# The pool for masked scores in the attention core: 15 tiles instead of 11

## The chip, the cores and the metric

The kernel runs on one core of one Trainium2 chip. The core has TensorE (PE, matmuls, with a weight load PEld ahead of each), VectorE (DVE), ScalarE (ACT), GpSimd (POOL) and SyncE (SP, which here issues the DMAs). The metric is the device time of one execution in microseconds, the median of several runs.

## What is computed

Two sequences, of 2048 and 256 rows of width 1024, go through two layers and a last RMS norm. The first layer is windowed attention, the second a bidirectional mLSTM. The change touches the attention alone. In the reference, cut to that:

```python
kb, vb = band(k), band(v)                       # the block's own 128 keys and both neighbours'
s = einsum('bnqgrd,bnkgd->bngrqk', qb, kb) * HEAD_DIM ** -0.5
s = where(mask, s, -inf)
m = maximum(max(s, axis=-1), sink)
p = exp(s - m)
den = sum(p, axis=-1) + exp(sink - m)
o = einsum('bngrqk,bnkgd->bnqgrd', p / den, vb)
y = (o * silu(z)) @ w_out
```

There are 16 query heads in 4 groups, 4 key heads, heads of 64, and blocks of 128 queries: 16 blocks for the first sequence, 2 for the second.

## The kernel before

The rows are 18 tiles of 128 (`NT`). `attn_core` works through them: `front(t)` projects tile `t` (keys and values in `kv`, queries in two halves in `q`; each is 24 matmuls of 128x512 in `project`, L471 to L473), turns keys and queries by the rope products (L1126, L1128, on VectorE), transposes them on TensorE (L528, L546) and splits them into two parts for exact products (`KH` and `KL`, `Q`). `core(t)` computes the attention of block `t` in three interleaved generators:

- `scores`: for each group of 4 heads, two matmuls per head write a score bank `s` in PSUM (L595, L596; 2 banks). VectorE adds the mask, writes the sum to a tile `Sm` in SBUF and leaves the row maximum (L598). Then `nm` and `es` (L603, L605), and ScalarE turns each `Sm` into its exponential in place (L609).
- `transposes`: TensorE transposes each 128x128 part of the four `Sm` of a group into a bank `ptp` (L622; 2 banks); ScalarE or VectorE copies it out to `PT` (L625; 4 tiles).
- `values`: TensorE multiplies `PT` with the values into a bank `o` (L634; 1 bank), ScalarE copies it out (L642) and SyncE stores it.

An `Sm` tile comes from a ring of `NSM` tiles. A block with both neighbours has 16 of them, each read by 3 transpositions; a tile is free again after the last of these. The lines:

```python
NSM = 11
...
Sm = p.tile([128, 3, 128], F32, tag="Sm", name="Sm", bufs=NSM)
nc.vector.tensor_tensor_reduce(Sm[:, :nk], S[:, :nk], mask[:, t % 3, win, :], 1.0, MASKED,
                               ALU.add, ALU.max, mx[:, c:c + 1])
...
nc.scalar.activation(Sg[c][:, :nk], Sg[c][:, :nk], AF.Exp, bias=nm[:, c:c + 1],
                     scale=HD ** -0.5, accum_out=rs[:, c:c + 1])
...
nc.tensor.transpose(tp[:, c, :], Ss[g][c][:, j, :], self.ident[:])
```

The strings `AORDER`, `AORDER1` and `AORDER2` say in which turn the generators of a block and the `front` of the block after next are written down. The order on each engine's queue is not that of the code, though: the kernel is recorded with a scheduler (`schedule_with_timeline_sim=True`, L1199) that reorders it while it hands out tiles, and a pool's size is one of the things that it goes by. Each engine then runs its queue in order.

After the attention core, `attn_gate` computes the gate `z`. Its weights `w_z` are loaded and split while the last blocks of the attention run (`part`, L193 and L194; `combinations`, L225 to L234); the first pair of its tiles is multiplied plainly (`plain`, L414 to L416, called Z here: 48 matmuls for the first halves, then 48 for the second).

Of the kernel before, what the change touches and what calls it, by code (L numbers as in the profile page):

```python
# [42 lines left out]
XOPS = ("a11", "s2", "a12", "s3", "s1", "a22", "s4")  # L43
WOPS = ("b11", "t2", "b21", "t3", "t1", "t4", "b22")
PAIRS = [(t, t + 1) for t in range(0, NT, 2)]
NSM = 11
NPT = 4
SPT = 18
AORDER = "fffssssfsffffppsvppv"
# [15 lines left out]
class Trunk:  # L65
# [422 lines left out]
    def attn_core(self):  # L488
        nc, tc, a = self.nc, self.tc, self.a
        with ExitStack() as st:  # L490
# [83 lines left out]
            def core(t):  # L574
# [9 lines left out]
                def scores():  # L584
                    for g in range(KVH):
                        mx = p.tile([128, 4], F32, tag="mx", name="mx", bufs=3)
                        Sg = []
                        for c in range(GRP):
# [7 lines left out]
                            nc.tensor.matmul(S[:, :nk, :], q, KL[:, g, win, :], start=False, stop=True)  # L596
                            Sm = p.tile([128, 3, 128], F32, tag="Sm", name="Sm", bufs=NSM)
                            nc.vector.tensor_tensor_reduce(Sm[:, :nk], S[:, :nk], mask[:, t % 3, win, :], 1.0, MASKED,  # L598
# [605 lines left out]
```

## Time and profile before

| | us |
|---|---|
| median of 3 runs | 2272.67 (2269.81 to 2273.28) |
| the profiled execution, its time | 2262.48 |
| its span | 2260.7 |
| TensorE busy | 2188.9 (97%) |
| VectorE busy | 1555.5 (69%) |
| ScalarE busy | 1163.0 (51%) |
| GpSimd busy | 462.1 (20%) |

The attention core takes the first 702 us of the span. The other 1558 us are the gate, the output projection, the mLSTM projections and its core. A busy share of TensorE is read with care: the end of a matmul is modelled and overlaps the start of the next, so its real pace is in the distance from start to start. In a row of several instructions ("x8"), the time is from the first start to the last end. A weight load (PEld) may run ahead of its matmul, so its idle time is not always lost time.

### The profile page before, as it was taken

The numbers are of one execution on the slowest core, as the hardware profiler recorded it, in microseconds if no ns is written. First come the engines' busy times: TensorE is split into PE (matmuls) and PEld (weight loads), VectorE is DVE, ScalarE is ACT, GpSimd is POOL, SyncE is SP. The second block draws the span as 40 slices with busy tenths as digits, with TensorE's granted clock in tenths as the row PEclk, the third lists the DMA queues.
The fourth block names the chain that finished last, engine by engine and source line by source line (L and its number), as shares of the span: only waits on it lengthen the run. The fifth ranks groups of instructions, "written<-read, shape, count | busy, mean of one in ns | idle before, by whom it ended". The sixth has DMA issues, their size and how long they took to land.

```text
span 2260.7 us, 34007 instructions
## 1 busy us (share of the span) xinstructions
PE 2188.9 (97%) x11342; PEld 1759.3 (78%) x11342; DVE 1555.5 (69%) x3437; ACT 1163.0 (51%) x2627; POOL 462.1 (20%) x410
## 2 busy tenths in 40 slices
PE   8999999999989999999999999999999987999998
PEld 7767676666666888788888899978887866888887
DVE  7565656566787779766855844676696677777784
ACT  6454545455565335556733732556474455455553
POOL 4212121212001221232000000023222235433320
PEclk9999999999999999999999999999999997999999
DMA  7111110111214446766854854655686565765642
GB/s 271 49 39 50 34 54 35 50 38 45 89 61 168 149 150 219 233 210 211 291 177 165 291 175 143 209 187 185 200 263 213 182 221 211 229 199 193 215 159 71
DMA packets 190160, 358.02 MB, mean 158 GB/s; under 512 B 20992, under 2 KB 23840, under 8 KB 189984
## 3 DMA queue, kind: packets, MB, share of 16 engines
q1 hardware_dynamic: 189840, 355.83, 47.5%
q8 instruction: 90, 1.47, 0.3%
q14 instruction: 86, 0.70, 0.1%
q10 hardware_dynamic: 144, 0.01, 0.0%
HBM read 258.48 MB, written 97.28 MB: 157 GB/s over the span
## 4 chain that ended last, share of the span: by engine, by line
PE 79%; DVE 8%; ACT 5%; DMA 4%; issue 2%; POOL 2%; SPq 0%; DVEq 0%; POOLq 0%; ACTq 0%
PE pj L471 6%; PE pj L473 6%; PE pj L472 6%; PE pj L297 4%; PE pj L299 4%; PE pj L298 4%; PE c L338 4%; PE pj L338 4%; PE ptp L622 3%; PE o L634 3%; PE c L297 3%; PE c L298 3%; PE c L299 3%; PE d L299 3%; PE d L298 3%; PE d L297 3%
## 5 line engine op out<-in xcount | busy, mean ns | idle before, releaser
L126 ACT CAST xhi<-rawx 128x512 fp32r<-128x512 f32 x396 | 243.7, 618 | 446.8 <-PE c L338 94.2
L127 DVE TENSOR_TENSOR xlo<-rawx,xhi 128x512 fp32r<-128x512 f32 x362 | 267.6, 743 | 94.7 <-ACT xhi L126 88.3
L471 PE MATMUL pj<-whi,xhi 128*128 128x512 f32 x720 | 294.5, 411 | 9.2 <-ACT whi L171 5.5
L473 PE MATMUL pj<-whi,xlo 128*128 128x512 f32 x720 | 283.7, 402 | 3.5 <-DVE xlo L127 3.5
L472 PE MATMUL pj<-wlo,xhi 128*128 128x512 f32 x720 | 285.6, 397 | 0.0
L609 ACT ACTIVATE Sm<-Sm,nm 128x384 f32<-128x384 f32 (+1 forms) x288 | 167.1, 582 | 95.1 <-DVE nm L603 88.7
L297 PE MATMUL pj<-whi,xhi 128*128 128x512 f32 x480 | 192.2, 400 | 4.9 <-ACT whi L193 3.4
L298 PE MATMUL pj<-wlo,xhi 128*128 128x512 f32 x480 | 190.3, 397 | 0.0
L299 PE MATMUL pj<-whi,xlo 128*128 128x512 f32 x480 | 190.0, 396 | 0.0
L598 DVE CUSTOM_DVE_ANT_0 Sm<-s,mask 128x384 f32<-128x384 f32 (+1 forms) x272 | 136.1, 530 | 73.1 <-PE s L596 70.0
L471 PEld LDWEIGHTS pj<-whi,xhi 128*128 128x128 f32 x720 | 136.1, 189 | 44.1 <-issue 8.8
L473 PEld LDWEIGHTS pj<-whi,xlo 128*128 128x128 f32 x720 | 136.1, 189 | 41.5 <-issue 6.5
L472 PEld LDWEIGHTS pj<-wlo,xhi 128*128 128x128 f32 x720 | 136.1, 189 | 30.4 <-issue 2.4
L622 PE MATMUL ptp<-ident,Sm 128*128 128x128 f32 x800 | 135.5, 280 | 10.5 <-DVE PT L625 7.1
L622 PEld LDWEIGHTS ptp<-ident,Sm 128*128 128x128 f32 x800 | 94.5, 141 | 55.0 <-ACT Sm L609 19.1
L297 PE MATMUL c<-whi,xhi 128*128 128x512 f32 x320 | 127.6, 399 | 0.0
L297 PE MATMUL d<-whi,xhi 128*128 128x512 f32 x320 | 127.3, 398 | 0.0
L298 PE MATMUL c<-wlo,xhi 128*128 128x512 f32 x320 | 127.3, 398 | 0.0
L299 PE MATMUL c<-whi,xlo 128*128 128x512 f32 x320 | 127.0, 397 | 0.0
L299 PE MATMUL d<-whi,xlo 128*128 128x512 f32 x320 | 126.8, 396 | 0.0
L298 PE MATMUL d<-wlo,xhi 128*128 128x512 f32 x320 | 126.1, 394 | 0.0
L595 PE MATMUL s<-KH,Q 128*128 128x384 f32 (+1 forms) x288 | 106.1, 380 | 10.2 <-DVE mx L598 4.5
(260 smaller groups left out, 5431.8 us busy)
## 6 DMA issues: line engine op xcount, KB each, us to landing
rawx<-xn2T SPq DMA_DIRECT2D x120, 256.0 KB, 3.1
x<-x SPq DMA_DIRECT2D x108, 256.0 KB, 4.5
rawx<-xsum SPq DMA_DIRECT2D x96, 256.0 KB, 2.8
rawx<-xT SPq DMA_DIRECT2D x72, 256.0 KB, 3.1
raww<-w_oz SPq DMA_DIRECT2D x64, 256.0 KB, 4.4
v<-v SPq DMA_DIRECT2D x36, 258.0 KB, 2.4
rawx<-v SPq DMA_DIRECT2D x36, 258.0 KB, 2.8
rawx<-x SPq DMA_DIRECT2D x36, 256.0 KB, 2.8
```

The costliest lines, as they stand in the source:

```text
L126: nc.scalar.copy(hi[:], src)
L127: (eng or nc.vector).tensor_sub(lo[:], src, hi[:].bitcast(F32))
L297: nc.tensor.matmul(o, xh, wh, start=i == 0 and not more, stop=False, skip_group_check=more)
L298: nc.tensor.matmul(o, xh, wl, start=False, stop=False, skip_group_check=more)
L299: nc.tensor.matmul(o, xl, wh, start=False, stop=i == 3, skip_group_check=more)
L338: nc.tensor.matmul(p, x, w[:, c0:c1], start=first and i + j == 0, stop=last and i == len(ws) - 1 and j == 2, skip_group_check=True)
L471: nc.tensor.matmul(o[:, :n], xh, wh, start=kt == 0, stop=False)
L472: nc.tensor.matmul(o[:, :n], xh, wl, start=False, stop=False)
L473: nc.tensor.matmul(o[:, :n], xl, wh, start=False, stop=kt == KT - 1)
L598: nc.vector.tensor_tensor_reduce(Sm[:, :nk], S[:, :nk], mask[:, t % 3, win, :], 1.0, MASKED, ALU.add, ALU.max, mx[:, c:c + 1])
L609: nc.scalar.activation(Sg[c][:, :nk], Sg[c][:, :nk], AF.Exp, bias=nm[:, c:c + 1], scale=HD ** -0.5, accum_out=rs[:, c:c + 1])
L622: nc.tensor.transpose(tp[:, c, :], Ss[g][c][:, j, :], self.ident[:])
```

## The change

One constant: `NSM`, the number of tiles in the ring for masked scores and their exponentials, goes from 11 to 15. A tile is 1536 bytes in each partition.

```diff
-NSM = 11
+NSM = 15
```

The four tiles add 6144 bytes per partition to the pool `a1`; the `PT` tiles and the pool with `KH`, `KL` and the mask behind it move up by as much. The scheduler makes another order of the attention core, from about 112 us on. TensorE's queue shows it. The first place is a block in the steady run, around 350 us in the trace of before. Names with numbers are buffers: `ptp_3682` is the first bank of transposed exponentials of one group (`Sm_3501` to `Sm_3516`), `s_3788`, `s_3793` and `s_3811` are score banks of the next block. Before:

```order
L622 MATMUL ptp_3682<-ident_60,Sm_3506 128x128
L595 MATMUL s_3788<-KH_283,Q_3200 128x384
L596 MATMUL s_3788<-KL_284,Q_3200 128x384
L595 MATMUL s_3793<-KH_283,Q_3200 128x384
L596 MATMUL s_3793<-KL_284,Q_3200 128x384
L622 MATMUL ptp_3682<-ident_60,Sm_3511 128x128
L595 MATMUL s_3811<-KH_283,Q_3200 128x384
L596 MATMUL s_3811<-KL_284,Q_3200 128x384
L622 MATMUL ptp_3682<-ident_60,Sm_3516 128x128
L622 MATMUL ptp_3696<-ident_60,Sm_3501 128x128
```

Single transpositions of one group alternate with score matmuls of the next block. The same transpositions on TensorE after the change:

```order
L622 MATMUL ptp_3682<-ident_60,Sm_3501 128x128
L622 MATMUL ptp_3682<-ident_60,Sm_3506 128x128
L622 MATMUL ptp_3682<-ident_60,Sm_3511 128x128
L622 MATMUL ptp_3682<-ident_60,Sm_3516 128x128
L622 MATMUL ptp_3689<-ident_60,Sm_3468 128x128
L622 MATMUL ptp_3689<-ident_60,Sm_3473 128x128
L622 MATMUL ptp_3689<-ident_60,Sm_3478 128x128
L622 MATMUL ptp_3689<-ident_60,Sm_3483 128x128
L473 MATMUL pj_3752<-whi_351,xlo_3735 128x512
L471 MATMUL pj_3752<-whi_357,xhi_3734 128x512
```

The four of a group stand together, and a projection follows; 23 instructions stand between the last of these transpositions and the bank `ptp_3696`, and the scores `s_3788` and `s_3793` come after that.

The second place is the end of the attention core, on TensorE, up to the first gate matmul. Before:

```order
L622 MATMUL ptp<-ident,Sm 128x128 x11
L634 MATMUL o<-PT,V 64x512 x2
L595 MATMUL s<-KH,Q 128x256
L596 MATMUL s<-KL,Q 128x256
L595 MATMUL s<-KH,Q 128x256
L596 MATMUL s<-KL,Q 128x256
L622 MATMUL ptp<-ident,Sm 128x128
L634 MATMUL o<-PT,V 64x512 x2
L622 MATMUL ptp<-ident,Sm 128x128 x15
L634 MATMUL o<-PT,V 64x512 x4
```

And the same end on TensorE after:

```order
L634 MATMUL o<-PT,V 64x512 x2
L622 MATMUL ptp<-ident,Sm 128x128 x4
L595 MATMUL s<-KH,Q 128x256
L596 MATMUL s<-KL,Q 128x256
L622 MATMUL ptp<-ident,Sm 128x128 x12
L634 MATMUL o<-PT,V 64x512 x2
L622 MATMUL ptp<-ident,Sm 128x128 x2
L634 MATMUL o<-PT,V 64x512 x2
L622 MATMUL ptp<-ident,Sm 128x128 x10
L634 MATMUL o<-PT,V 64x512 x4
```

More transpositions and all value products of the last block now stand behind the last score. VectorE's queue at the same end, before:

```order
L615 RECIPROCAL den<-rs 128x4
L194 TENSOR_TENSOR wlo<-raww,whi 128x512
L625 COPY PT<-ptp 128x512
L194 TENSOR_TENSOR wlo<-raww,whi 128x512 x3
L225 SCALAR_TENSOR_TENSOR raww<-raww,g 128x512
L625 COPY PT<-ptp 128x512
```

And VectorE's queue there after:

```order
L625 COPY PT<-ptp 128x512
L614 TENSOR_TENSOR rs<-rs,es 128x4
L615 RECIPROCAL den<-rs 128x4
L625 COPY PT<-ptp 128x512 x2
L127 TENSOR_TENSOR xlo<-rawx,xhi 128x512 x2
L194 TENSOR_TENSOR wlo<-raww,whi 128x512 x3
L225 SCALAR_TENSOR_TENSOR raww<-raww,g 128x512
```

The last copies to `PT` now stand ahead of the weight splits (L194, L225), which followed and preceded them before. On ScalarE the last copy to `PT` and four casts of weights (L193) change places in the same way.

## Rows read from the trace of the kernel before

**Rows 1.** The page: the span, and part 1.

```profile
span 2260.7 us, 34007 instructions
PE 2188.9 (97%) x11342; PEld 1759.3 (78%) x11342; DVE 1555.5 (69%) x3437; ACT 1163.0 (51%) x2627; POOL 462.1 (20%) x410
```

**Rows 2.** Stretches: length, busy time by engine (instructions), granted clock, DMA share, GB/s.

```profile
165.00:280.00 115.00, 112.17 (x563) 77.91 (x562) 69.60 (x212) 58.12 (x163) 20.79 (x18) 1.00 0.14 44
...
600.00:656.00 56.00, 49.61 (x248) 33.95 (x246) 50.96 (x127) 37.27 (x96) 4.18 (x3) 1.00 0.40 127
656.00:702.00 46.00, 38.99 (x199) 22.66 (x197) 31.81 (x126) 32.80 (x107) 0.00 (x0) 0.90 0.15 52
...
700.00:750.00 50.00, 49.95 (x227) 39.59 (x226) 38.23 (x56) 20.75 (x34) 10.12 (x9) 0.97 0.64 212
```

**Rows 3.** Line 598: ns shortest/median/longest; then VectorE's idle time before it.

```profile
L598 DVE CUSTOM_DVE_ANT_0 Sm<-s,mask x272: 415/553/559, 45.6 to 691.4; 128x384 f32<-128x384 f32 x112, 128x256 f32<-128x256 f32 x24
...
  PE ptp L622: 2.0, 4
```

**Rows 4.** Weight loads' waits, 45 to 600 us: total, times, longest.

```profile
PEld ptp L622 <- ACT Sm L609: 12.5, 24, 0.8
...
PEld s L595 <- DVE mx L598: 11.3, 28, 0.8
...
PEld s L595 <- ACT KH L530: 10.4, 13, 1.3
```

**Rows 5.** Timeline: start, us, engine, line, operation, tiles [idle before and releaser].

```profile
341.66 0.27 PE L622 MATMUL ptp<-ident,Sm 128*128 128x128 f32 x1
341.69 0.42 PE L595 MATMUL s<-KH,Q 128*128 128x384 f32 x1
...
350.51 0.27 PE L622 MATMUL ptp<-ident,Sm 128*128 128x128 f32 x1
...
350.99 0.44 PE L595 MATMUL s<-KH,Q 128*128 128x384 f32 x1 [0.20 <-DVE mx L598]
...
351.21 0.66 DVE L625 COPY PT<-ptp 128x512 f32<-128x512 f32 x1
...
351.44 0.27 PE L622 MATMUL ptp<-ident,Sm 128*128 128x128 f32 x1
...
352.02 1.25 PE L622 MATMUL ptp<-ident,Sm 128*128 128x128 f32 x8 [0.31 <-DVE PT L625]
```

**Rows 6.** The chain that ended last: start, us, engine, line and count.

```profile
108.12 0.87 PE ptp L622 x8
...
275.15 1.24 PE ptp L622 x8
...
390.34 1.24 PE ptp L622 x8
```

**Rows 7.** Timeline of the handover, TensorE.

```profile
612.98 0.66 PE L622 MATMUL ptp<-ident,Sm 128*128 128x128 f32 x4 [1.52 <-DVE PT L625]
```

**Rows 8.** Timeline of the tail, VectorE and TensorE.

```profile
667.16 0.36 PE L595 MATMUL s<-KH,Q 128*128 128x256 f32 x1 [1.77 <-DVE Q L552]
...
696.38 0.69 DVE L625 COPY PT<-ptp 128x512 f32<-128x512 f32 x1
...
697.12 1.11 PE L622 MATMUL ptp<-ident,Sm 128*128 128x128 f32 x4 [1.20 <-DVE PT L625]
...
700.18 0.29 PEld L634 LDWEIGHTS o<-PT,V 128*64 128x64 f32 x4 [1.73 <-DVE PT L625]
```

**Rows 9.** The tail's clock: stretches as in rows 2, and TensorE's timeline.

```profile
694.00:696.00 2.00, 1.36 (x7) 0.69 (x6) 0.57 (x3) 2.00 (x8) 0.00 (x0) 1.00 0.12 44
...
698.00:700.00 2.00, 2.00 (x6) 0.29 (x4) 2.00 (x4) 0.00 (x0) 0.00 (x0) 0.50 0.48 161
...
679.98 2.07 PE L622 MATMUL ptp<-ident,Sm 128*128 128x128 f32 x11
698.16 4.00 PE L634 MATMUL o<-PT,V 128*64 128x512 f32 x8
```

## The prediction

> **What bounds the kernel now.** I read the page's first lines, then the stretches, then who waits for whom, then single instructions. TensorE is busy for 2188.9 of 2260.7 us [rows 1], so a change that only moves work can win no more than TensorE's waits. The pool at issue lives in the attention core, up to 702 us. The reader should see three stages there [rows 2]. In the steady stage (blocks 1 to 14) TensorE is nearly full, 112.17 of 115.00 us, while VectorE (69.60) and ScalarE (58.12) have room. In the handover (600 to 656 us) VectorE is the full one, 50.96 of 56.00, because the weights of the next stage (`w_z`) are split into parts there. In the tail (656 to 702 us) the projections have run out: TensorE has no filler left and is busy 38.99 of 46.00, with VectorE and ScalarE at about 32. After 702 us it is full again, so what is saved before that point is saved for good.
>
> Busy time hides waits, because the shown end of a matmul overlaps the next start. So I laid the starts of the trace over the built order, one instruction on one, and called a wait what an interval has above the usual interval of that pair of kinds. Eight transpositions in a row take 0.87 us, 0.109 each [rows 6]. From a transposition to a score matmul it is usually 0.03 us (341.66 to 341.69), but 0.48 from 350.51 to 350.99: a wait of 0.45. From transposition to transposition, 351.44 to 352.02, it is 0.47 too much [rows 5]. The first waits for the maximum that VectorE makes of an earlier score bank, the second for the copy that empties a `ptp` bank and starts only at 351.21 [rows 5]. The pattern comes back every three blocks, 275.15 to 390.34, which is 115.2 us [rows 6], with 11 waits over 0.15 us, 4.7 us together. From 112 us, where the two orders part, to 600 us there are some 28 us of such waits, small ones included; in the handover 10, in the tail 15.
>
> **What the pool itself makes wait.** VectorE idled before its masked maximum (L598) for only 2.0 us, 4 times, because a transposition still had to release the `Sm` tile [rows 3]. So the missing tiles are hardly seen as waits. They act through the order: laying out the built order, 64 of 277 scores stand on TensorE ahead of the transposition that frees their `Sm` tile before the change, 11 of 273 after it. With 11 tiles, scores and transpositions must alternate closely; with 15, a group of scores goes ahead and its transpositions come later, in fours, with projections between.
>
> **The change part by part.** Instructions: none is added or removed on TensorE in this stage (800 transpositions, 576 score matmuls, 200 value matmuls, 1296 of the projections in both orders). A change of kind from one matmul to the next costs a little too, so the order could matter by itself. Summed with the usual intervals of each pair of kinds, both orders come to 640 us from the start to the end of the first gate pair, 0.5 us apart, so nothing is won or lost by the packing. All of the gain must be waits.
>
> *Steady stage.* I sorted every TensorE instruction that reuses a bank, or reads a fresh exponential, by how much TensorE work lies between it and the one that it depends on, and took the measured waits of each class in the trace of before:
> - transposition into a bank last written 1.0 to 1.5 us of work earlier: 18 of them, 5.6 us of waits; 3 after the change. Saved: 15 x 0.31 = 4.7.
> - the same under 1.0 us: 12, 1.4 us; 6 after. Saved 0.7.
> - score into a bank used less than 0.8 us earlier: 42, 7.8 us; 26 after. Saved 16 x 0.186 = 3.0.
> - score at 1.5 to 2.0 us: 27, 5.1 us; 18 after. Saved 1.7.
> - transposition of an exponential within 3 us of its group's last score: 36, 1.5 us; 8 after. Saved 1.1.
>
> That is 11.2 us; I take **10**, because some scores of the third class only moved within it. Larger distances hold almost no wait in before. Bounds: 4, if only the first class goes and the scores wait again elsewhere; 18, if the larger distances take the small waits too. The row nearest to what remains is the score that waits for VectorE, 11.3 us of weight-load idle in 28 places, against 12.5 us in 24 places for ScalarE's exponentials [rows 4]; the second kind is what the extra tiles take away, so I stay in the middle.
>
> [...] I leave it 0.04, below the range.
>
> *Handover.* The longest wait is for a copy behind weight splits in VectorE's queue, 1.52 us [rows 7]. VectorE's work there is unchanged and it has 5 us free [rows 2]. Bounds 0 and 5; I take **1**.
>
> *Tail.* Here the end is changed: before it, VectorE's queue has four L194 and an L225 ahead of the last copies, and ScalarE four casts (L193) ahead of one. TensorE's transpositions wait 1.20 us for the copy that starts at 696.38, and the weight load of the last values 1.73 us for the one after it [rows 8]. After the change the copies stand ahead of that work. The cover of the moved work is the second half of the gate pair, 48 matmuls that need none of it, and VectorE is then busy 38.23 of 50 us [rows 2], so I cost it at nothing; without that cover it is 4 x 0.7 + 0.8 = 3.6 us. The wait of 1.77 us for the last `Q` at 667.16 [rows 8] stays: it hangs on the last projections. I take **3**, with bounds of -3 (the scores that now run ahead delay copies) and 8 (half of the 15 us).
>
> Other queues: SyncE's loads of `xT` and of `x` swap places by one or two issues, and GpSimd's halves likewise, both with a block to spare. Past 702 us the orders are almost the same. The larger pool moves `PT`, `KH` and `KL` up by 6 KB per partition, under the buffers of the following stages; those are first written after the last score, so I cost it at nothing. If one were needed earlier it would cost one split, 0.7 us.
>
> **Sum.** 10 + 1 + 3 = 14 us: 2262.5 becomes 2248.5 for the profiled execution. That one is 10.2 us faster than the median shown, 2272.7; the saving should be the same there, so 2258.7.
>
> **The rivals.**
> *No change.* The waits move instead of going, because a block's chain (maximum, exponential, transposition, copy) is as long as before and two score banks still pace it. For it: score banks and their maxima hold the score matmuls most often [rows 4]. Against it: VectorE and ScalarE have over 40 us free in 115 [rows 2], so they do not pace the stage. Time: 2272.7, within 4.5 us.
>
> *Slower.* Scores that run ahead fill VectorE's queue with maxima of 0.55 us [rows 3]; the rope products of the block after next stand behind them, its keys come late, and the first score of a block waits. The place is the first score after each key transposition, 14 blocks. The price is at most the longest wait of that kind in before, 1.3 us in the row of waits for `KH` [rows 4]: 14 x 1.3 = 18, less 13 saved, gives 5 us slower, 2278. It decides from some 1 us of new waiting a block. Against it: in the built order the distance from projection to key transposition is over 8 us in nearly all blocks, as before.
>
> [...]
>
> That the change does nothing is excluded by the built order.
>
> **How the numbers follow.** A saving of 8 to 24 us: 0.62. The clock's partial loss or a smaller steady saving, 4.5 to 8 us: 0.11. No change: 0.18. Slower: 0.09. A measurement of this kernel can tell about 0.2%, 4.5 us, from no change. So faster 0.73, same 0.18, slower 0.09. Range: 2272.7 - 24 = 2249 (18 for the steady stage, 1 and 5) up to 2274, just past no change; about 0.07 lies below and 0.13 above.
>
> **What would show it.** In the profile after, the transposition's waits for copies (L622 for L625) and for exponentials (L609) in the steady stage should fall by more than half, the waits of scores for maxima by a third, and the distance between the first gate matmul and the start should shrink by 10 us before 600 us. The last value matmuls should come without a wait behind L194. I am wrong if score waits (L595) grow by what the transpositions lose, if the waits for `KH` reach 1 us a block, or if the clock falls earlier in the tail.

## The result, and the profile after

The change makes the kernel 0.8% faster: 2249.21 us, median of 4 runs (2248.49 to 2249.59), against 2271.59 us for the kernel before, measured beside it (4 runs, 2269.81 to 2273.28). The ratio is 0.9917, 95% interval 0.9901 to 0.9933. In a later comparison it was 2248.59 against 2267.83, 0.9913 (0.9891 to 0.9936). So the saving is 22 and 19 us, where 14 were forecast. 2249.21 lies inside the range, 2249 to 2274, by 0.2 us, and 2248.59 lies just outside: that the first falls inside is luck. The profiled execution took 2249.23 us, 13.25 under that of the kernel before.

The page of the profile of the kernel after, the span and part 1, to be laid beside [rows 1]:

```profile
span 2247.2 us, 34017 instructions
PE 2181.7 (97%) x11342; PEld 1761.3 (78%) x11342; DVE 1552.6 (69%) x3437; ACT 1162.4 (52%) x2627; POOL 461.7 (21%) x410
```

Every engine has as many instructions of work as before, and busy time is nearly the same. TensorE's busy time fell by 7.2 us (2188.9 less 2181.7) with the same instructions; a shown end overlaps the next start (in the row at 347.69 below, 1.08 us shown and 1.01 to the next start), so part of the waits is probably counted in it.

Where the time went is seen best in where a stage begins. The gate's line L414 makes the first halves of the gate pair before and during the tail (`pj`) and the second halves behind it (`c`); L297 is the next pair's multiplication. Single lines of the trace, before and after: engine, tile and count, shortest, median and longest ns, then the first and the last start. The kernel before:

```profile
L414 PE MATMUL pj<-whi,xhi x80: 388/396/477, 642.2 to 1677.4; 128*128 128x512 f32 x80
L414 PE MATMUL c<-whi,xhi x80: 389/395/797, 702.1 to 1683.0; 128*128 128x512 f32 x80
L297 PE MATMUL pj<-whi,xhi x480: 387/395/794, 714.8 to 1843.9; 128*128 128x512 f32 x160
```

And the kernel after:

```profile
L414 PE MATMUL pj<-whi,xhi x80: 389/396/498, 631.3 to 1657.3; 128*128 128x512 f32 x80
L414 PE MATMUL c<-whi,xhi x80: 388/395/503, 684.7 to 1662.9; 128*128 128x512 f32 x80
L297 PE MATMUL pj<-whi,xhi x480: 387/394/628, 696.0 to 1826.6; 128*128 128x512 f32 x160
```

The first gate product starts 10.9 us earlier, the second halves 17.4, the next pair 18.8. So the attention core and the gate pair give 18.8 us. In the profiles the rest, from there to the end, runs 1545.9 us before (2260.7 less 714.8) and 1551.2 after. The orders there are almost the same, so the 5.3 us that the profiled execution gave back were not expected; the experiments come back to them.

Stretches of the kernel after, with the columns of [rows 2]: the steady stage, the handover, the tail, and 50 us behind the tail.

```profile
155.00:270.00 115.00, 112.98 (x572) 79.33 (x570) 70.08 (x210) 58.39 (x163) 20.86 (x18) 1.00 0.14 46
...
590.00:646.50 56.50, 53.23 (x268) 38.74 (x267) 54.69 (x134) 40.27 (x94) 5.80 (x4) 0.97 0.41 127
646.50:684.70 38.20, 33.41 (x190) 20.86 (x188) 25.33 (x114) 28.79 (x100) 0.00 (x0) 0.96 0.09 35
684.70:734.70 50.00, 50.00 (x234) 40.70 (x233) 43.29 (x63) 24.07 (x40) 10.82 (x9) 1.00 0.70 232
```

In 115 us of the steady stage TensorE now starts 572 instructions where it started 563. The tail is 38.2 us long instead of 45.2 (656.9 to 702.1). In the handover VectorE is full to 97%, where it was at 91%, and TensorE is 94% busy against 89%. TensorE's granted clock in the handover is 0.97, where it was 1.00; the experiments come to that too.

The counted waits, made in the prediction's way (an interval between two starts on TensorE, less what that pair of kinds usually takes), give the same picture. The steady stage here is the stretch with equal TensorE work in all kernels, from 107 to 553 us of that work, counted from the start. How large a wait comes out depends on what is taken as usual (the prediction found 28 us with the small ones, this count 34.1), so the differences between kernels are what counts:

| waits of TensorE, us | before | after |
|---|---|---|
| steady stage: scores | 12.1 in 44 | 7.8 in 27 |
| transpositions | 9.8 in 56 | 4.1 in 27 |
| other | 6.3 in 36 | 6.3 in 34 |
| split value pairs (below) | none | 5.7 in 12 |
| small intervals, under 0.05 each | 5.8 | 3.1 |
| steady stage, all | 34.1 | 26.9 |
| handover | 11.4 | 6.5 |
| tail | 15.1 | 9.8 |

Three stages give 7.2, 4.9 and 5.3 us, 17.4 together; 1.4 more lie ahead of the steady stage, behind the tail and in the changed mix of kinds.

The 5.7 us in one row are new. A value pair is two products of 64 output columns each, two passes of each: four in all. This is TensorE's timeline in the kernel after, with start, duration, line and count, first for a pair whose four passes stand together:

```profile
347.69 1.08 PE L634 MATMUL o<-PT,V 128*64 128x512 f32 x4
348.70 0.44 PE L595 MATMUL s<-KH,Q 128*128 128x384 f32 x1
```

And a pair that the order split, with four transpositions of queries between the halves:

```profile
221.22 1.07 PE L634 MATMUL o<-PT,V 128*64 128x512 f32 x2
222.22 0.66 PE L546 MATMUL pqt<-ident,t 128*128 128x128 f32 x4
222.81 1.07 PE L634 MATMUL o<-PT,V 128*64 128x512 f32 x2
223.81 0.66 PE L622 MATMUL ptp<-ident,Sm 128*128 128x128 f32 x4
```

Four passes together hold TensorE 1.01 us (347.69 to 348.70). Two passes alone hold it 1.00 us (221.22 to 222.22), and so do the other two (222.81 to 223.81). Each product is 64 columns wide (`128*64` in its rows, where the other matmuls of the attention core have `128*128`). In this trace two of them ran side by side where they stood next to each other, and nowhere else: in all 94 adjacent pairs the passes start in twos, 0.006 to 0.008 us apart, and in each of the 12 halves of split pairs the two passes start 0.48 us apart. A split pair costs about 1 us more, by these intervals. Why a product needs the neighbour was not shown. The kernel before has no split pair, the kernel after has 6, all in the steady stage: 6 x 0.95 = 5.7 us.

### The profile page after: what moved, and what is told of

Its sections match the earlier page's. It is cut to its first block, busy times and chain, and to the rows that moved or that the text cites. A ratio compares the mean times of both kernels' runs of the same rounds, so it can differ in the third digit from the quotient of the medians.

```text
span 2247.2 us, 34017 instructions
## 1 busy us (share of the span) xinstructions
PE 2181.7 (97%) x11342; PEld 1761.3 (78%) x11342; DVE 1552.6 (69%) x3437; ACT 1162.4 (52%) x2627; POOL 461.7 (21%) x410
## 4 chain that ended last, share of the span: by engine, by line
PE 79%; DVE 9%; DMA 4%; ACT 3%; issue 2%; POOL 2%; SPq 0%; DVEq 0%; POOLq 0%; ACTq 0%
PE pj L471 6%; PE pj L473 6%; PE pj L472 6%; PE pj L297 5%; PE pj L298 5%; PE pj L299 5%; PE o L634 4%; PE c L338 4%; PE pj L338 4%; PE ptp L622 3%; PE c L297 3%; PE c L298 3%; PE c L299 3%; PE d L297 3%; PE d L299 3%; PE d L298 3%
## 5 line engine op out<-in xcount | busy, mean ns | idle before, releaser
L297 PE MATMUL pj<-whi,xhi 128*128 128x512 f32 x480 | 191.7, 399 | 5.0 <-ACT whi L193 2.8
L598 DVE CUSTOM_DVE_ANT_0 Sm<-s,mask 128x384 f32<-128x384 f32 (+1 forms) x272 | 137.5, 529 | 70.9 <-PE s L596 67.5
L297 PE MATMUL c<-whi,xhi 128*128 128x512 f32 x320 | 127.6, 399 | 0.0
L297 PE MATMUL d<-whi,xhi 128*128 128x512 f32 x320 | 127.6, 399 | 0.0
L625 DVE COPY PT<-ptp 128x512 f32<-128x512 f32 x128 | 87.2, 687 | 50.3 <-PE ptp L622 46.4
```

The costliest lines, as they stand in the source:

```text
L297: nc.tensor.matmul(o, xh, wh, start=i == 0 and not more, stop=False, skip_group_check=more)
```

## The experiments

Each kernel is timed beside the kernel before on the same chip. The gain is that of the medians against the kernel before in the same comparison; the medians of before differ by up to 5.6 us between comparisons. "Next pair" is the first start of L297 in the profile. Waits are counted as above, in us.

| kernel | us | gain | ratio (95%) | next pair | steady, handover, tail | split pairs |
|---|---|---|---|---|---|---|
| before (11 tiles) | 2271.59, 2267.53, 2266.01, 2267.83 | | | 714.8 | 34.1, 11.4, 15.1 | 0 |
| e8_ring_12 | 2255.07 | 10.9 | 0.9947 (0.9928 to 0.9965) | 700.9 | 25.3, 10.8, 11.3 | 2 |
| e7_ring_13 | 2245.39 | 20.6 | 0.9913 (0.9893 to 0.9932) | 692.4 | 22.0, 8.0, 11.4 | 1 |
| e4_ring_14 | 2236.40 | 31.1 | 0.9863 (0.9837 to 0.9890) | 686.2 | 17.6, 7.7, 9.5 | 0 |
| after (15), e10_after_timed | 2248.59 | 19.2 | 0.9913 (0.9891 to 0.9936) | 696.0, 695.2 | 26.9, 6.5, 9.8 | 6 |
| e1_pairs_kept (15) | 2243.12 | 24.4 | 0.9891 (0.9860 to 0.9921) | 689.3 | 21.2, 10.2, 8.5 | 0 |
| e9_ring_14_pairs_kept | 2246.29 | 21.5 | 0.9909 (0.9879 to 0.9938) | 693.5 | 22.4, 10.5, 11.9 | 0 |
| e2_tail_only | 2259.47 | 8.1 | 0.9964 (0.9951 to 0.9977) | 704.0 | 34.1, 7.8, 9.3 | 0 |
| e3_steady_only | 2251.85 | 15.7 | 0.9926 (0.9898 to 0.9955) | 697.5 | 24.4, 8.1, 13.0 | 5 |

### Is the profile the same twice?

The kernel before, and the kernel after, each profiled once more.

> The kernel before, unchanged, profiled once more. Its profiled execution took 2262.5 us, while its timed runs lie between 2259 and 2273 us. Theory: the attention core takes the same time in every execution (first gate pair done at 714 to 716 us), and the difference between executions lies after it. Rival: the profiled execution had a lucky attention core; then the gate pair ends up to 10 us later here.

> The kernel after the change, unchanged, profiled once more. Theory: the attention core ends as in the first profile of it (first gate pair done at 695 to 697 us), 18.8 us before that of before; the stretch after it varies by some us. Rival: the 18.8 us contain luck, and it comes out 3 us or more away.

> The change itself, timed beside the kernel before on this chip. Theory: 2247 to 2250, 18 to 20 us under the kernel before. Rival (the 22 us of the first comparison is the size): 22 us or more. The attention core should again end within 0.5 us of the two profiles seen, first gate product of the next pair at 696.0.

The core repeats: the counted waits of before are 34.2, 11.4 and 15.0, those of after 26.9, 6.5 and 9.7. The next pair starts at 714.4 in the second profile of before, and at 696.0 and 695.2 in the later two of after (the last 0.8 off, where 0.5 was expected; the median, 2248.59, is 19.2 under the kernel before, as expected). The first two lines are of the second profile of before, the third of the second profile of after:

```profile
L297 PE MATMUL pj<-whi,xhi x480: 387/394/632, 714.4 to 1840.9; 128*128 128x512 f32 x160
L338 PE MATMUL pj<-whi,xhi x256: 276/280/392, 1259.0 to 1457.6; 128*128 128x256 f32 x128
```

```profile
L297 PE MATMUL pj<-whi,xhi x480: 387/394/792, 696.0 to 1827.7; 128*128 128x512 f32 x160
```

The 0.8 us go with the clock in the handover. In the first profile of after it falls for a while at 612 us, in the third it does not. The same 6 us of the first and of the third, granted clock behind the five engines' busy times:

```profile
611.00:617.00 6.00, 5.05 (x26) 4.06 (x26) 5.92 (x18) 5.09 (x15) 0.00 (x0) 0.72 0.59 178
611.00:617.00 6.00, 5.01 (x31) 3.16 (x31) 5.93 (x18) 5.25 (x15) 0.00 (x0) 1.00 0.49 160
```

What follows the core does not repeat as well as the core does. In the first profile of before, L338 began at 1262.2, 547.4 us after the next pair; in the second at 1259.0, 544.6 after it. From the last L297 to the end it is 408.0 in the one (1852.7 to 2260.7) and 411.2 in the other (1849.7 to 2260.9). In that end part TensorE's clock is low for a while in each of these profiles. This is 1855 to 1895 us of the first profile of before:

```profile
1855.00:1895.00 40.00, 21.53 (x88) 17.83 (x88) 31.86 (x48) 26.14 (x67) 28.17 (x21) 0.62 0.82 299
```

And the same 40 us of the second, with 11 instructions more:

```profile
1855.00:1895.00 40.00, 22.31 (x99) 18.14 (x99) 25.64 (x52) 24.11 (x63) 25.48 (x20) 0.69 0.79 280
```

That is a shift in time, not more or less of the low clock: from 1850 to 2235 us both are granted 0.96, and the execution with 0.69 here has the longer end part. So the clock does not explain its 3.2 us.

```profile
1850.00:2235.00 385.00, 360.51 (x1961) 309.57 (x1960) 291.39 (x698) 205.48 (x564) 139.47 (x117) 0.96 0.58 198
1850.00:2235.00 385.00, 357.61 (x1947) 306.72 (x1946) 283.60 (x694) 204.46 (x561) 135.22 (x116) 0.96 0.58 195
```

What this stretch has besides is a long wait of TensorE, by the trace one for a load (`kT`): 11.0 us in the first profile of after (the first profile of before shows 9.6 us there and another releaser). The row of the first profile of after:

```profile
PE s L990 <- DMA kT<-kT: 11.0, 1, 11.0
```

How much of the time behind the core hangs on it was not tried.

The rest of the program takes 1545.9 and 1546.5 us in the two profiles of before, and 1551.2, 1549.8 and 1549.6 in the three of after. So the profiles of after show 3 to 5 us given back behind the core, and their totals are 13 to 16 us under those of before, while the medians differ by 19 and 22, which is about the gain of the core alone. The timed runs of before lie between 2259.25 and 2275.79 us, and both of its profiles, 2262.48 and 2262.64, near the low end; the runs of after lie between 2246.73 and 2249.59. Why the later stages of before vary more, and whether its profiled executions were luckily placed there, is open: no profile of a run at 2272 us exists.

### What does a split pair cost?

The change, with a high priority for the value products. It was meant for the second product of each pair alone (L639), so that it follows the first at once. But `half(j, 1)`, which issues the first, is called inside the same `with`, behind `high_priority()`, so both products of the pair have it:

```diff
-                            with tc.issue_after(half(j, 1).ins):
+                            with tc.high_priority(), tc.issue_after(half(j, 1).ins):
```

> The kernel after the change with one thing more: the second value matmul of a pair is given a high priority, so that it always follows the first at once. In the order after the change 6 of the 100 pairs of value matmuls are split (another instruction stands between the two), before none; in the trace after, each half of a split pair takes 0.47 us more, 12 x 0.47 = 5.6 us. Theory (the longer ring lowers waits, and split pairs take a part of it back): 5 us faster than after, 25 us faster than before. Rival (TensorE would have waited there anyhow, so a split costs nothing): within 1.5 us of after, 20 us faster than before.

The split pairs are gone, the core ends 6.7 us earlier than in the change (689.3 against 696.0), and the medians say 5.5 to 6.1 (2243.12 against 2248.59 and 2249.21); by the gains, 24.4 against 19.2 and 22.4, it is 2.0 to 5.2. That fits the 5 us expected, and not the rival by which a split costs nothing. But the order is another one, and not the split alone moved: transpositions and scores waited 4.5 us less, while values waited 7.1 us instead of 2.7, since both products of a pair now stand ahead of the copies that they need. So these 6.7 us are the net of several terms; the price of a split is read from the intervals above. Weight loads' waits in the steady stage of this kernel, total, times and longest:

```profile
PEld o L634 <- DVE PT L625: 8.9, 11, 1.4
...
PEld s L595 <- DVE mx L598: 6.3, 17, 1.5
```

One of those waits in its timeline, where the copy starts at 274.99 and the pair 0.75 us later:

```profile
274.99 0.69 DVE L625 COPY PT<-ptp 128x512 f32<-128x512 f32 x1
...
275.74 1.08 PE L634 MATMUL o<-PT,V 128*64 128x512 f32 x4 [1.09 <-DVE PT L625]
```

### Which stage gives the gain?

The four extra tiles given to one window alone, as a ring of their own for the fourth head of each group: first from block 14 on, then up to block 13. The ring for the other three heads keeps its 11 tiles.

```diff
-NSM = 15
+NSM = 11
...
-Sm = p.tile([128, 3, 128], F32, tag="Sm", name="Sm", bufs=NSM)
+Sm = p.tile([128, 3, 128], F32, tag="Sx" if c == 3 and t >= 14 else "Sm", name="Sm", bufs=4 if c == 3 and t >= 14 else NSM)
```

> Ring of 11, but in the last four blocks (14 to 17) the fourth head of each group takes its tile from a ring of 4 more; the order of the steady stage stays that of before. Theory (each stage gains by its own order): the tail and the handover gain 9 us, the steady stage nothing, so 9 us faster than before. Rival A (the gain comes from the end alone, where the last copies stand ahead of the weight splits): nearly all of it, 17 to 22 us faster. Rival B (the tail's waits hang on the last projections and on the clock): within 3 us of before.

The second kernel has `t < 14` in both places.

> The four extra tiles for the fourth head of each group in blocks 0 to 13 alone; from block 14 the ring has 11. Theory: the steady stage loses 10 us of waits and the handover 3, and 5 split pairs of value matmuls give some 5 us back: 8 us faster than before, and with the tail-only kernel's 9 it adds up to the change's. Rival A (the end alone): within 3 us of before. Rival B (the two halves don't add up, since one order brings forth the other): 15 us or more faster.

The first did what was expected: no gain in the steady stage (34.1 us of waits, as before), 3.6 less in the handover, 5.8 less in the tail, 8.1 on the median. The second missed: 15.7 instead of 8, which is what its rival B said. Its steady stage gained 9.7 us in spite of five split pairs, and the handover (3.3) and the tail (2.1) gained as well, although the ring of the last blocks has its old size. So the stages are not independent: what the scheduler has done up to block 13 also changes how the rest comes out. "The tail's gain" is a property of an order, not only of the tiles there. The sum of the halves, 24 us against 19 to 22, says nothing on this: the intervals are wider than the difference, and a separate ring for one head is not the change's common ring of 15.

### How does the gain go with the number of tiles?

One number changed in each: `NSM` at 12, 13 and 14.

> A ring of 12 tiles. Theory (distances in the order that comes out; two split pairs): 9 us less in the steady stage, 5 in the handover, 5 in the tail, less 2 for the split pairs: 17 us faster than before. Rival (the gain grows with the tiles): a third of the gain of 14 tiles, 8 to 10 us.

> A ring of 13 tiles. Theory (distances in the order that comes out, and split pairs: one here): the classes give 8 us less waiting in the steady stage, 6 in the handover, 3 in the tail, less 1 for the split pair and 2 more up to the gate pair's end: 18 us faster than before. Rival (the gain grows with the tiles, 31 us at 14): 15 to 21 us cannot tell the two apart, but under 12 or over 25 us speaks against both.

> A ring of 14 tiles in place of 11. Theory (what counts is the order that comes out: distances between dependent instructions, and split pairs): the distances are about those of 15 tiles and no pair is split, so 3 to 6 us faster than after, 22 to 26 faster than before. Rival (the gain grows with the tiles): three quarters of the gain, 15 us faster than before, 5 us slower than after.

The gains are 10.9, 20.6 and 31.1 us, some 10 for each tile, and 19 to 22 at 15. Twelve missed: 10.9 instead of 17, near the linear rival's 8 to 10, though its core won 13.9. Its profiled execution, the slowest of its four, needed 1556.6 us from the next pair to the end, 10 more than before. Thirteen was as expected, in a band that cannot tell the theory from its rival. Fourteen was better than expected, 31.1 instead of 22 to 26, and beats both kernels: 2236.40 us, 0.9863 of before, and 9 to 13 us under the change (9 to 12 by the gains, 12 to 13 by the medians). Its waits are the lowest in sum: 17.6 in the steady stage, of which transpositions 1.7 and values 1.1, and no split pair. From the page of the profile of the kernel with 14 tiles:

```profile
span 2235.8 us, 33997 instructions
PE 2172.1 (97%) x11342; PEld 1759.4 (79%) x11342; DVE 1545.9 (69%) x3437; ACT 1161.4 (52%) x2627; POOL 456.9 (20%) x410
```

### Why 14 beats 15 with the pairs kept

e1 has no split pair and is still 7 us behind 14 tiles. Either pulling the values forward costs that, or the fifteenth tile does. So the edit of e1, with both products of a pair raised, was put on 14 tiles, where it has no split to mend:

```diff
-NSM = 15
+NSM = 14
...
-                            with tc.issue_after(half(j, 1).ins):
+                            with tc.high_priority(), tc.issue_after(half(j, 1).ins):
```

> 14 tiles, and the second product of each value pair issued at once behind the first, as in e1_pairs_kept. With 14 tiles alone no value pair is split in the built order, so keeping pairs together has nothing to win here; what it changes is only that the values stand earlier in TensorE's queue. Theory (the gap of 7 us between e1_pairs_kept and e4_ring_14 is the price of pulling the values forward: they wait for the copy of their exponentials, 7.1 us in e1 against 1.1 in e4): 3 to 6 us slower than e4_ring_14, about 2240, and value products that wait for PT for some 5 us more in the steady stage. Rival (pulling forward costs nothing, and 15 tiles are worse than 14 for another reason): within 2 us of e4_ring_14, 2236.

The values wait for `PT` 6.7 us instead of 1.1, as the theory said, and the price is larger than it said: the core ends 7.3 us later (693.5 against 686.2), the median is 9.9 higher (9.6 by the gains). TensorE's own waits from 45 to 590 us, first of this kernel:

```profile
PE o L634 <- DVE PT L625: 5.9, 7, 1.1
PE s L595 <- DVE mx L598: 1.9, 5, 0.7
```

Then of 14 tiles alone:

```profile
PE s L595 <- DVE mx L598: 4.0, 12, 0.6
PE o L634 <- DVE PT L625: 0.9, 1, 0.9
```

So the edit that mends the pairs costs about as much as it mends. A priority for the second product alone was not built. With the edit, 15 tiles end the core earlier than 14 do (689.3 against 693.5), and the median is 3 us lower, with intervals that overlap: the fifteenth tile by itself does no harm that these runs show. The core of 14 tiles ends 9.8 us before that of the change. Its steady stage waits 9.3 us less: 5.7 are the split pairs by their rows, another 4.0 are transpositions and values that wait less (1.7 and 1.1 against 4.1 and 2.7), and the other rows give 0.4 back. The handover takes 1.2 more, the tail 0.3 less. What an order with 15 tiles, whole pairs and no forced place would take was not tried.

## Why the prediction was right, and where it was not

**What bounds the kernel, and the reading by intervals: right.** The gain came out of TensorE's waits before the second gate halves, with no change in its work. The tiles are hardly waited for themselves: VectorE's idle time for an `Sm` tile, [rows 3], was 2.0 us in 4 places, and after the change it is in the last of these lines (VectorE's idle time ahead of L598):

```profile
L598 DVE CUSTOM_DVE_ANT_0 Sm<-s,mask x272: 392/552/560, 46.2 to 676.5; 128x384 f32<-128x384 f32 x112, 128x256 f32<-128x256 f32 x24
...
  PE ptp L622: 2.6, 3
```

The visible wait did not even fall, and 18.8 us were won. Who looks only for waits on the ring would have found nothing to win. That they act through the order is shown in part: `e1` and `e9` leave the rings as they are, change the order, and move the core by 6.7 and 7.3 us. A larger ring also moves other tiles in SBUF, and no kernel has the new order with the old ring, so a share of that move is not excluded.

**Steady stage, 10 us: right in the waits, wrong in the sum.** The counted waits fell from 28.3 to 18.1 us, by 10.2. Transpositions fell by 58% ("more than half"), scores by 36%. TensorE's own idle rows say by whom it was held. Before (45 to 600 us):

```profile
PE ptp L622 <- DVE PT L625: 3.4, 11, 0.3
PE s L595 <- DVE mx L598: 3.3, 17, 0.2
PE s L595 <- ACT KH L530: 2.4, 5, 0.9
```

And after (45 to 590 us):

```profile
PE s L595 <- DVE mx L598: 3.5, 10, 0.7
```

The first and the third row have no counterpart after. The waits for maxima, which were to fall by "a third", did not fall in this list; what fell for the scores are those for `KH`. The list of weight loads in the kernel after, to be laid beside [rows 4]:

```profile
PEld s L595 <- DVE mx L598: 17.6, 28, 1.4
...
PEld ptp L622 <- ACT Sm L609: 6.4, 12, 0.8
PEld o L634 <- DVE PT L625: 3.2, 3, 1.4
PEld ptp L622 <- DVE PT L625: 3.1, 6, 0.8
...
PEld s L595 <- ACT KH L530: 0.8, 1, 0.8
```

The exponentials went from 12.5 us in 24 places to 6.4 in 12, and the waits for `KH` from 10.4 in 13 to 0.8 in 1. But the scores' row rose from 11.3 to 17.6, where "I am wrong if score waits grow" was written. TensorE's counted score waits fell nevertheless, by 4.3: the idle time of the weight loads is not that of the matmuls. The distance from start to start decides, as the prediction read it.

What failed is the sentence that nothing is won or lost by the packing, a term put at nothing. A change of kind does cost: in the trace of before, from 107 to 600 us, a value product starts 0.20 us behind a transposition (median of 57) and another transposition 0.11 us (of 457). The sum of usual intervals did come out equal (640.6 and 640.1 us), but the usual interval behind a value product was that of a whole pair. Split pairs were in the built order to be seen, 0 before and 6 after, and gave back 5.7 us. With small intervals gaining 2.7 besides (5.8 to 3.1), the stage's term is 7.2 instead of 10.

**Handover, 1 us: mis-sized, 4.9.** I had seen VectorE's 5 us of room and not that the new order uses it: VectorE now runs at 97%, and TensorE's waits there fell to 6.5. The upper bound, 5, was the right value. The clock, which fell there at 612 us in the first profile of after and not in the third (0.72 and 1.00 granted from 611 to 617 us), went with about 0.8 us given back.

**Tail, 3 us: mis-sized, 5.3, and one of its two waits misread.** The named mechanism is there in part. The end of the attention core in the kernel after, to be laid beside [rows 8]:

```profile
681.93 0.69 DVE L625 COPY PT<-ptp 128x512 f32<-128x512 f32 x1 [1.62 <-PE ptp L622]
...
682.26 0.66 PE L622 MATMUL ptp<-ident,Sm 128*128 128x128 f32 x4 [0.37 <-ACT PT L625]
682.85 1.94 PE L634 MATMUL o<-PT,V 128*64 128x512 f32 x8
...
683.70 0.20 PEld L634 LDWEIGHTS o<-PT,V 128*64 128x64 f32 x4 [0.66 <-DVE PT L625]
...
684.71 0.50 PE L414 MATMUL c<-whi,xhi 128*128 128x512 f32 x1
```

The copy finds VectorE idle for 1.62 us, where L194 stood ahead of it, and the transpositions' wait of 1.20 is 0.37. The 1.73 us of [rows 8] are 0.66 now, but they were idle time of the weight load and hardly TensorE's: from 698.16 to the gate product at 702.1 the eight passes held TensorE 3.9 us, and two pairs at a granted clock of 0.50 (698 to 702 us) need, by an estimate from the 1.01 us of a pair at 1.00, 4 x 1.01 = 4.0. That half of the term had next to nothing to win. What these passes did win is the clock, which I had as a risk only: they took 4.00 us at a granted clock of 0.50 [rows 9] and now take 1.94 at 1.00. The wait for the last `Q` stayed, as forecast: 1.8 us in both traces. The rest of the 5.3 is not taken apart.

**The clock's partial loss: not seen at the end.** No run shows the loss that the 0.11 allowed for. In the profile after, the end kept a granted clock of 1.00 with its runs of transpositions; the clock stands behind the five engines' busy times:

```profile
672.00:678.00 6.00, 5.20 (x35) 3.04 (x33) 4.38 (x25) 5.55 (x22) 0.00 (x0) 1.00 0.10 37
678.00:684.00 6.00, 5.63 (x33) 2.51 (x33) 2.42 (x5) 3.46 (x12) 0.00 (x0) 1.00 0.17 65
```

The 33 instructions of the last 6 us are all transpositions and value passes. Value passes stand between the runs, so what transpositions alone do to the clock was not shown. The clock did fall earlier in the tail once, at 656.7 us (0.50 in 658 to 660), which I had named as a sign against me; before, it fell at 669.2 (0.50 in 670 to 672) and again at 696.6 (0.50 in 698 to 700). So the tail has less of it, not more: 0.96 granted from 646.5 to 684.7 us against 0.90 from 656 to 702.

**No change, and slower: not seen.** The two score banks do not hold the stage at its old pace. The waits for `KH` that were to grow to 1 us a block fell to 0.8 us in one place.

**The 0.04, below the range.** No run shows nearly all of the steady waits gone: at 15 tiles 7.2 of 34.1 us went, at 14 tiles 16.5. The time at 14 tiles, 2236.40, lies below the range all the same. A time there deserved more than 0.04.

**The median.** "The saving should be the same there" was a step of its own, and wrong: the median saved 22.4 us where the profiled execution saved 13.25, and 19.2 in the later comparison, while the second profiles of the two kernels differ by 14.9. The profiled execution of before was quick behind the core, and what is saved before 702 us was not "saved for good" in the profiles. By terms, 14 forecast became 18.8: steady -2.8, handover +3.9, tail +2.3, the rest of the core +1.4. That the profiled execution saved 13.25 us, so near the 14 forecast, is luck: it is 18.8 less the 5.3 given back behind the core. The remaining 3.6 of 22.4 come from what follows the core and from the base.

## What to carry to other kernels

Where a scheduler writes the order, the size of a ring is an input of the scheduler, and its gain is neither seen in waits on that ring nor steady in its size: build several sizes, compare the orders, and time the neighbours (here 14 beat 15 by 9 to 13 us). When two orders are compared by usual intervals, look first for neighbours that run side by side while adjacent (here four passes of two adjacent value products in 1.01 us, two passes of one alone in 1.00); counting split pairs would have priced this order better. And take the gain of one stage from where the next stage starts, in two profiles of each kernel, since what comes behind can move by several us by itself.

## What was not expected of the hardware

A value product of 64 columns takes 1.00 us for its two passes when alone (221.22 us in the profile after), and two of them 1.01 us for all four when adjacent (347.69). The low-clock stretch after the last L297 lies elsewhere in time in two executions of one and the same kernel (0.62 and 0.69 granted in the same 40 us, 0.96 in both from 1850 to 2235 us), and the time from the last L297 to the end differs by 3.2 us (408.0 and 411.2), the longer one with the 0.69.
